# Gate and up as a 2x2x2 block product with seven products, and a down projection that is fed through DRAM

## The chip, the cores and the metric

The kernel runs on one core of a Trainium2 chip. The metric is the device time of one execution in microseconds (us); a lower one is better. The engines are TensorE (PE, matmuls), VectorE (DVE), ScalarE (ACT), GpSimd (POOL) and SyncE (SP, which here only issues DMAs). Each runs its own instructions in order, and they wait for each other by semaphores.

## The reference

One layer of a hybrid decoder, for a batch of one, 1024 tokens, width 1024, in float32. An input projection feeds four heads of a gated delta rule and four heads of differential attention; both results go through one output projection and are added to the residual x. Then comes the feed-forward part that the change is about:

```
x2  = x + concat(la, diff) @ w_out
h   = rmsnorm(x2, ffn_norm_w)
gu  = h @ w_gate_up                 # 1024 x (2 * 2816): gate, then up
act = silu(gu[:, :2816]) * gu[:, 2816:]
x3  = x2 + act @ w_down             # 2816 x 1024
out = rmsnorm(x3, final_norm_w)
```

## The kernel before

Every float32 matrix product is made of three matmuls on operands that are split into a rounded high part and the low rest (`mm3`: high by high, high by low, low by high). The high part is a cast on ACT, the low part a subtraction on DVE, in some places on POOL in two halves (`split`).

The hidden width of 2816 is 22 blocks of 128, called f here. Tokens are eight blocks of 128, called t; k counts eight blocks of the width of 1024; u and n are halves of 512 columns.

Ahead of the FFN: the output projection is done in units of 128 tokens by 512 columns (`out_unit`, 12 matmuls and one DVE sum into the residual, L769). The residual x2 lies in SBUF for all tokens, loaded from x in four DMAs of 1 MB (L796). The units of the delta heads (16) and the diff units of the tokens 4 to 7 are woven into the attention by `fill`, a generator which the attention code asks for matmuls where PE would wait. The diff units of the tokens 0 to 3 follow after the attention (`unit_d`). Each finished half of a token block is squared on ACT (`half_h`), the normalised row block xn is made by two DVE scalings (L1044), transposed by PE and split into `hT_h` and `hT_l` (`trans_h`, L189).

The FFN: `gate_up(f)` loads 128 columns of gate and of up, splits them and does 48 matmuls for each, over all eight k and both halves of the tokens, into two 1024-wide PSUM tiles (`big`). Then come Silu on ACT, the product with up on DVE (L1114) and the split of the result (L1116, L1117), which stays in SBUF. After each group of f blocks (one, then nine twos and a last three; `cuts`) the down products of that group are done: for each t and n, three matmuls per f into a 512-wide PSUM tile (`sm` or `fl`, taken in turn, two buffers each), and a DVE sum into x2 (L1141). In the last group the final norm follows each token block.

PSUM has two `big`, two `sm` and two `fl` buffers. SBUF tiles come from named pools with a number of buffers, so an instruction that fills a buffer waits for the last reader of what was in it. DMAs are issued by SP, in order.

## Time and profile before

| | |
|---|---|
| median of three runs | 1415.88 us (1414.29 to 1417.27) |
| profiled execution | 1417.17 us, of which the span is 1415.5 us |
| mean granted PE clock | 0.987 of full speed |
| busy PE, DVE, ACT, POOL | 1356.0, 665.5, 417.2, 146.7 us |
| matmuls and transpositions on PE | 6804 |
| HBM read, written | 83.48 MB, 18.88 MB |

The span is the part between the first and the last instruction. A busy time is the union of an engine's instructions. Matmuls overlap in the pipeline, so their distance from start to start says what one costs, not the duration in its row. In rows of groups, "idle before" is the time that the engine stood still just before these instructions, with what ended it.

### The profile page before, as it was taken

To read this page: it belongs to the slowest core of one execution; us is meant where nothing else is said; L and a number is where in the kernel's file an instruction comes from. 1 tells how busy PE (TensorE), PEld (TensorE's weight loads), DVE (VectorE), ACT (ScalarE), POOL (GpSimd) and SP (SyncE) were. 2 spreads that over 40 slices of the span, in tenths; PEclk is the share of its full clock that TensorE was granted. 3 is DMA by queue.
4 is the path that set the end of the run, shared out by engine and by line. 5 is a ranking of instruction groups with operands and counts; after the bars stand their busy time and mean duration, and the time that the engine had idled before them with its cause. 6 is when DMAs were issued, how large, how long until landed. Compare 5 with 4: busy or idle time off the path is not lost.

```text
span 1415.5 us, 16570 instructions
## 1 busy us (share of the span) xinstructions
PE 1356.0 (96%) x6804; PEld 1138.5 (80%) x6804; DVE 665.5 (47%) x1071; ACT 417.2 (29%) x758; POOL 146.7 (10%) x124
## 2 busy tenths in 40 slices
...
DMA packets 109108, 103.43 MB, mean 73 GB/s; under 512 B 12096, under 2 KB 89192, under 8 KB 109032
## 3 DMA queue, kind: packets, MB, share of 16 engines
...
q14 instruction: 23, 0.19, 0.0%
HBM read 83.48 MB, written 18.88 MB: 72 GB/s over the span
## 4 chain that ended last, share of the span: by engine, by line
PE 78%; DVE 9%; DMA 5%; issue 3%; ACT 2%; POOL 2%; SPq 0%; POOLq 0%; DVEq 0%; ACTq 0%
PE big L142 15%; PE big L143 15%; PE big L144 15%; PE fl L142 5%; PE fl L144 5%; PE fl L143 5%; PE sm L144 3%; PE sm L143 3%; PE sm L142 3%; DMA ks<-cv 2%; DMA w_raw<-in_w_out 1%; DVE tmp L507 1%; DVE av L509 1%; PE fl L542 1%; DVE mx L888 1%
## 5 line engine op out<-in xcount | busy, mean ns | idle before, releaser
L142 PE MATMUL big<-hT_h,w_h 128*128 128x512 f32 x704 | 274.0, 389 | 0.0
L144 PE MATMUL big<-hT_h,w_l 128*128 128x512 f32 x704 | 273.9, 389 | 0.0
L143 PE MATMUL big<-hT_l,w_h 128*128 128x512 f32 x704 | 273.9, 389 | 0.0
L149 ACT CAST w_h<-w_raw 128x1024 fp32r<-128x1024 f32 x76 | 79.9, 1053 | 404.6 <-PE big L143 223.2
L143 PEld LDWEIGHTS big<-hT_l,w_h 128*128 128x128 f32 x704 | 132.2, 188 | 27.4
L142 PEld LDWEIGHTS big<-hT_h,w_h 128*128 128x128 f32 x704 | 132.2, 188 | 27.3
L144 PEld LDWEIGHTS big<-hT_h,w_l 128*128 128x128 f32 x704 | 132.2, 188 | 27.3
L151 DVE TENSOR_TENSOR w_l<-w_raw,w_h 128x1024 fp32r<-128x1024 f32 x56 | 69.5, 1240 | 156.6 <-ACT w_h L149 138.3
L142 PE MATMUL big<-xT_h,w_h 128*128 128x512 f32 x320 | 127.5, 398 | 0.7 <-DVE cv L433 0.7
L144 PE MATMUL big<-xT_h,w_l 128*128 128x512 f32 x320 | 127.0, 398 | 0.5 <-DVE w_l L151 0.5
L143 PE MATMUL big<-xT_l,w_h 128*128 128x512 f32 x320 | 126.3, 395 | 0.0
L1114 DVE TENSOR_TENSOR cv<-big,cv 128x1024 f32<-128x1024 f32 x22 | 26.9, 1224 | 206.4 <-PE big L144 206.4
L149 ACT CAST dn_h<-w_raw 128x1024 fp32r<-128x1024 f32 x22 | 23.1, 1052 | 235.8 <-PE sm L144 182.2
L1141 DVE TENSOR_TENSOR x<-fl,x 128x512 f32<-128x512 f32 x88 | 60.6, 689 | 40.9 <-PE fl L144 40.9
L155 POOL TENSOR_TENSOR w_l<-w_raw,w_h 128x512 fp32r<-128x512 f32 x40 | 54.5, 1387 | 243.7 <-ACT w_h L149 243.7
L1141 DVE TENSOR_TENSOR x<-sm,x 128x512 f32<-128x512 f32 x88 | 60.6, 688 | 36.5 <-PE sm L144 36.1
L1149 POOL TENSOR_TENSOR ssn<-ssn,expo 128x1 f32<-128x1 f32 x8 | 4.4, 551 | 702.8 <-DVE ssn L1147 702.8
L142 PEld LDWEIGHTS big<-xT_h,w_h 128*128 128x128 f32 x320 | 60.9, 190 | 13.9 <-issue 2.2
L144 PEld LDWEIGHTS big<-xT_h,w_l 128*128 128x128 f32 x320 | 60.6, 189 | 13.1 <-DVE w_l L151 1.0
L143 PEld LDWEIGHTS big<-xT_l,w_h 128*128 128x128 f32 x320 | 60.6, 189 | 12.2 <-issue 0.2
L142 PE MATMUL fl<-dn_h,av 128*128 128x512 f32 x176 | 69.7, 396 | 0.0
L143 PE MATMUL fl<-dn_l,av 128*128 128x512 f32 x176 | 68.6, 390 | 0.0
...
## 6 DMA issues: line engine op xcount, KB each, us to landing
w_raw<-in_w_gate_up SPq DMA_DIRECT2D x44, 512.0 KB, 3.9
w_raw<-in_w_in SPq DMA_DIRECT2D x24, 512.0 KB, 4.0
w_raw<-in_w_down SPq DMA_DIRECT2D x22, 512.0 KB, 3.6
xt<-in_x SPq DMA_DIRECT2D x8, 512.0 KB, 5.5
ks<-cv ACTq DMA_DIRECT2D x8, 512.0 KB, 12.5
aqh<-qh SPq DMA_DIRECT2D x16, 256.0 KB, 4.9
aql<-ql SPq DMA_DIRECT2D x16, 256.0 KB, 7.3
...
```

The costliest lines, as they stand in the source:

```text
L142: nc.tensor.matmul(ps, lhsT=lh, rhs=rh, start=start, stop=False)
L143: nc.tensor.matmul(ps, lhsT=lh, rhs=rl, start=False, stop=False)
L144: nc.tensor.matmul(ps, lhsT=ll, rhs=rh, start=False, stop=stop)
L149: nc.scalar.copy(out=h, in_=raw)
L151: nc.vector.tensor_tensor(out=l, in0=raw, in1=h.bitcast(F32), op=ALU.subtract)
L155: eng.tensor_tensor(out=l[:, c], in0=raw[:, c], in1=h[:, c].bitcast(F32), op=ALU.subtract)
L507: nc.vector.tensor_tensor(out=tv, in0=B[:, i + 1:, i:i + 1].broadcast_to([P, nr, ncol]), in1=X[:, i:i + 1, :ncol].broadcast_to([P, nr, nco ...
L509: nc.vector.tensor_tensor(out=X[:, i + 1:, :ncol], in0=X[:, i + 1:, :ncol], in1=tv, op=ALU.subtract)
L542: nc.tensor.matmul(ps[:, jj * P:(jj + 1) * P], lhsT=At[:, b0 + jj, :], rhs=Df[:, half * 4 + jj, :], start=True, stop=True)
L888: nc.vector.tensor_reduce(out=mx[:, m:m + 1], in_=s[:, :, :w], axis=AX.XY, op=ALU.max, negate=True)
L1114: nc.vector.tensor_tensor(out=sg, in0=ups, in1=sg, op=ALU.mult)
L1141: nc.vector.tensor_tensor(out=x2[:, t, ns], in0=ps, in1=x2[:, t, ns], op=ALU.add)
```

## The change

**Gate and up.** The two matrices and h are cut into blocks: A11 and A12 are the gate weights for the lower and upper half of k, A21 and A22 the up weights; B has rows for the halves of k and columns for the halves of the tokens. Seven products of half size (`product`, 12 matmuls each: four k by three) stand for eight: A11 by B11, A12 by B21, and five on sums, S1 by T1, S2 by T2, S3 by T3, S4 by B22, A22 by T4. The sums T1 to T4 of h are formed once, in `trans_h`; S1 to S4 of the weights in each f on DVE (`w_sum`), one f ahead (`w_prepare`), and two of the low parts on POOL. Two products are accumulated into the PSUM tile of another; the rest are added on DVE (`add`: u2, u3, and the sums into tg and tu). One `big` tile now holds two 512-wide results, pc and pd.

**Down.** The activation of f is stored to DRAM (`act_dr`), in place of being split. When all 22 are done, `down_load` brings activation and down weights back, splits both, and the down products run in seven chunks of 2, 2, 3, 4, 4, 4 and 3 blocks. The first chunk copies PSUM into x2 on ACT, in the third POOL adds the residual, which comes from DRAM; the final norm in the last chunk is as before.

**Residual.** It is no longer held in SBUF. For each unit of the delta heads 128x512 is loaded from x (`res_load`), added and stored to DRAM (`x2_dr`); the diff units load it for a token block (`x2_load`), add, and `half_h` stores it again. The diff units of the tokens 4 to 7 now run token by token.

The core of the diff:

```diff
...
+    def out_unit(parts, mix, u, t, ps, res):
...
+        nc.vector.tensor_tensor(out=res, in0=ps, in1=res, op=ALU.add)
...
+    def res_load(t, u):
+        xh = late["x2p"].tile([P, 512], F32, name="xh", bufs=4)
+        nc.sync.dma_start(out=xh, in_=x_d[t * P:(t + 1) * P, u * 512:(u + 1) * 512])
+        return xh
...
+    def x2_load(t):
+        x2t[t] = op.tile([P, T], F32, name="avl", bufs=4)
+        nc.sync.dma_start(out=x2t[t], in_=x2_dr[t])
...
-        for t in range(0, NT, 2):
-            nc.sync.dma_start(out=x2[:, t:t + 2, :], in_=x_d[t * P:(t + 2) * P, :].rearrange("(t p) d -> p t d", p=P))
...
+        units = [(t, u) for u in range(2) for t in range(NT)]
+        res = {units[0]: res_load(*units[0]), units[1]: res_load(*units[1])}
+        wd = late["wd"] = []
+        for n, (t, u) in enumerate(units):
...
+            yield from out_unit(w[u], mix_la, u, t, flr(), res[t, u])
+            if n + 2 < len(units):
+                res[units[n + 2]] = res_load(*units[n + 2])
+            if n:
+                pt_, pu = units[n - 1]
+                nc.sync.dma_start(out=x2_dr[pt_][:, pu * 512:(pu + 1) * 512], in_=res.pop((pt_, pu)))
+        nc.sync.dma_start(out=x2_dr[t][:, u * 512:(u + 1) * 512], in_=res.pop((t, u)))
...
+        for t in range(4, NT):
+            if t < NT - 2:
+                x2_load(t + 2)
+            for u in range(2):
+                yield from out_unit(wd[u], mix_d, u, t, flr(), x2t[t][:, u * 512:(u + 1) * 512])
...
+            pool, name, bufs = (wp, "w_raw", 2) if t in (4, 5) else (wpools[1][0], "w_raw", 1) if t == 6 else (op, "avl", 4)
+            xns[t] = pool.tile([P, T], F32, name=name, bufs=bufs)
...
+        nc.sync.dma_start(out=x2_dr[t], in_=x2t.pop(t))
+
+    def parts(h, l, raw, eng):
+        nc.scalar.copy(out=h, in_=raw)
+        eng.tensor_tensor(out=l, in0=raw, in1=h.bitcast(F32), op=ALU.subtract)
...
+        pt = big()
...
+        ptv = pt.rearrange("p (k c) -> p k c", c=P)
+        lo, hi = ptv[:, 0:HALF, :], ptv[:, HALF:NK, :]
+        cs = slice((t % 4) * P, (t % 4 + 1) * P)
+        if t >= 4:
+            f = kept[t] = cvt().rearrange("p (k c) -> p k c", c=P)
+            b12, t3 = f[:, 0:HALF, :], f[:, HALF:NK, :]
+            nc.scalar.copy(out=b12, in_=lo)
+            parts(B22[0][:, :, cs], B22[1][:, :, cs], hi, nc.vector)
+            nc.vector.tensor_tensor(out=t3, in0=hi, in1=b12, op=ALU.subtract)
+            parts(T3[0][:, :, cs], T3[1][:, :, cs], t3, nc.gpsimd)
+            return
+        f = kept.pop(t + 4)
+        f1, f2, f4 = f[:, 0:HALF, :], f[:, HALF:NK, :], scratch()
+        nc.scalar.copy(out=first[0][:, :, cs], in_=ptv)
+        nc.vector.tensor_tensor(out=f1, in0=f1, in1=lo, op=ALU.subtract)
+        nc.vector.tensor_tensor(out=f2, in0=lo, in1=f2, op=ALU.add)
+        nc.vector.tensor_tensor(out=first[1][:, :, cs], in0=ptv, in1=first[0][:, :, cs].bitcast(F32), op=ALU.subtract)
+        nc.vector.tensor_tensor(out=f4, in0=hi, in1=f2, op=ALU.subtract)
+        parts(T1[0][:, :, cs], T1[1][:, :, cs], f1, nc.gpsimd)
+        parts(T2[0][:, :, cs], T2[1][:, :, cs], f2, nc.vector)
+        parts(T4[0][:, :, cs], T4[1][:, :, cs], f4, nc.vector)
...
+    def operand():
+        pool, name = slots[used[0] % 4]
+        used[0] += 1
+        w = pool.tile([P, T], F32R, name=name, bufs=4).rearrange("p (a k c) -> p a k c", a=2, c=P)
+        return w[:, 0], w[:, 1]
...
+    def w_fetch(f):
+        rg = wp.tile([P, NK, P], F32, name="w_raw", bufs=2)
+        nc.sync.dma_start(out=rg, in_=gu_v[:, :, f * P:(f + 1) * P])
+        ru = wpools[1][0].tile([P, NK, P], F32, name="w_raw", bufs=1)
+        nc.sync.dma_start(out=ru, in_=gu_v[:, :, DFF + f * P:DFF + (f + 1) * P])
+        return rg[:, 0:HALF], rg[:, HALF:NK], ru[:, 0:HALF], ru[:, HALF:NK]
+
+    def w_split(raw, eng):
+        hl = operand()
+        parts(*hl, raw, eng)
+        return hl
+
+    def w_sum(a0, a1, alu):
+        r = scratch()
+        nc.vector.tensor_tensor(out=r, in0=a0, in1=a1, op=alu)
+        return r
...
+                yield W
+        a11, a12, a21, a22 = w_fetch(f)
+        W["A11"] = w_split(a11, nc.vector)
+        yield W
+        s1 = w_sum(a21, a22, ALU.add)
+        W["S1"] = w_split(s1, nc.vector)
+        yield W
+        yield W
+        s2 = w_sum(s1, a11, ALU.subtract)
+        s4 = w_sum(a12, s2, ALU.subtract)
+        W["S2"] = w_split(s2, nc.vector)
+        yield W
+        W["S4"] = w_split(s4, nc.gpsimd)
+        yield W
+        W["S3"] = w_split(w_sum(a11, a21, ALU.subtract), nc.gpsimd)
+        yield W
+        W["A12"] = w_split(a12, nc.vector)
+        W["A22"] = w_split(a22, nc.vector)
+        yield W
...
+    def product(ps, w, b, begin):
+        for k in range(HALF):
+            for n, (x, y) in enumerate(((w[0], b[0]), (w[0], b[1]), (w[1], b[0]))):
+                nc.tensor.matmul(ps, lhsT=x[:, k, :], rhs=y[:, k, :], start=begin and k == 0 and n == 0,
+                                 stop=k == HALF - 1 and n == 2, skip_group_check=not begin)
...
+    def gate_up(f, W, nxt):
+        pa, pb, pc, pd = banks()
+        tx, tg, tu = temps()
+        u2, u3 = tx[:, n0], tx[:, n1]
+        product(pa, W["A11"], B11, True)
+        nc.scalar.copy(out=u2, in_=pa)
+        next(nxt)
+        product(pb, W["S2"], T2, True)
+        add(u2, pb, u2)
+        next(nxt)
+        product(pc, W["S3"], T3, True)
+        add(u3, pc, u2)
+        next(nxt)
+        product(pd, W["S1"], T1, True)
+        add(tu[:, n1], pd, u3)
+        next(nxt)
+        product(pa, W["A12"], B21, False)
+        nc.scalar.activation(out=tg[:, n0], in_=pa, func=AF.Silu)
+        next(nxt)
+        product(pd, W["S4"], B22, False)
+        add(tg[:, n1], pd, u2)
+        nc.scalar.activation(out=tg[:, n1], in_=tg[:, n1], func=AF.Silu)
+        nc.gpsimd.tensor_tensor(out=tg[:, n1], in0=tg[:, n1], in1=tu[:, n1], op=ALU.mult)
+        next(nxt)
+        product(pc, W["A22"], T4, False)
+        add(tu[:, n0], pc, u2)
+        nc.vector.tensor_tensor(out=tg[:, n0], in0=tg[:, n0], in1=tu[:, n0], op=ALU.mult)
+        W = next(nxt)
+        nc.sync.dma_start(out=act_dr[f], in_=tg)
+        return W
...
+    x2_load(2)
+    unit_d(1, 0)
+    unit_d(1, 1)
+    trans_h(0)
+    W0["S3"] = w_split(w_sum(a11, a21, ALU.subtract), nc.gpsimd)
+    x2_load(3)
+    unit_d(2, 0)
+    unit_d(2, 1)
+    trans_h(1)
+    s4 = w_sum(a12, a22, ALU.subtract)
+    nc.vector.tensor_tensor(out=s4, in0=s4, in1=a21, op=ALU.subtract)
+    nc.vector.tensor_tensor(out=s4, in0=s4, in1=a11, op=ALU.add)
+    W0["S4"] = w_split(s4, nc.gpsimd)
+    unit_d(3, 0)
+    unit_d(3, 1)
+    trans_h(2)
...
+    product(pc, W0["S3"], T3, True)
+    trans_h(3)
+    product(pd, W0["S4"], B22, True)
+    nc.scalar.copy(out=tg[:, n1], in_=pd)
+    late_operands()
+    nxt = w_prepare(1)
+    product(pa, W0["A11"], B11, True)
+    nc.scalar.copy(out=u2, in_=pa)
+    product(pd, W0["S1"], T1, True)
+    next(nxt)
+    product(pb, W0["S2"], T2, True)
...
+    def down_load(f):
+        pool, nh, nl, bufs = homes[min(f % 9, 4)]
+        out = []
+        for src in (act_dr[f], w_dn[f * P:(f + 1) * P, :]):
+            raw = cvt() if f > 1 and src is not act_dr[f] else wp.tile([P, T], F32, name="w_raw", bufs=2)
+            nc.sync.dma_start(out=raw, in_=src)
+            h = pool.tile([P, T], F32R, name=nh, bufs=bufs)
+            l = pool.tile([P, T], F32R, name=nl, bufs=bufs)
+            parts(h, l, raw, nc.vector)
+            out += [h, l]
+        down[f] = out
+
+    for f in range(1, NF):
+        W = gate_up(f, W, w_prepare(f + 1))
+        if f in (4, 6):
+            down_load(f // 2 - 2)
...
+    close_hp()
...
+    chunks = [(0, 2), (2, 4), (4, 7), (7, 11), (11, 15), (15, 19), (19, NF)]
+    ready = 2
+    for c, (f0, f1) in enumerate(chunks):
+        while ready < f1:
+            down_load(ready)
+            ready += 1
+        ahead = chunks[c + 1][1] if c + 1 < len(chunks) else NF
...
+            if c == 2:
+                xr = cvt()
+                nc.sync.dma_start(out=xr, in_=x2_dr[t])
+                for ns in (n0, n1):
+                    nc.gpsimd.tensor_tensor(out=x2[:, t, ns], in0=x2[:, t, ns], in1=xr[:, ns], op=ALU.add)
...
+                for f in range(f0, f1):
+                    ah, al, dh, dl = down[f]
+                    mm3(ps, ah[:, ts], al[:, ts], dh[:, ns], dl[:, ns], f == f0, f == f1 - 1)
+                if c == 0:
+                    nc.scalar.copy(out=x2[:, t, ns], in_=ps)
+                else:
+                    add(x2[:, t, ns], ps, x2[:, t, ns])
...
+            if t % 2 == 1 and ready < ahead:
+                down_load(ready)
+                ready += 1
...
```

In the order of the built program, three places. First PE in gate and up, one f in the middle. Before, the last matmuls of gate and the first of up, in two `big` tiles:

```order
L142 MATMUL big_6430<-hT_h_5502,w_h_6426 128x512
L143 MATMUL big_6430<-hT_l_5503,w_h_6426 128x512
L144 MATMUL big_6430<-hT_h_5502,w_l_6427 128x512
L142 MATMUL big_6496<-hT_h_5502,w_h_6492 128x512
L143 MATMUL big_6496<-hT_l_5503,w_h_6492 128x512
L144 MATMUL big_6496<-hT_h_5502,w_l_6493 128x512
```

Now, from the end of S3 (operand hT3) over four matmuls of A12 (operand hB1, tile sm) to S1 (hT1):

```order
L1177 MATMUL big_6516<-hT3_h_5591,cv_6492 128x512 x2
L1177 MATMUL big_6516<-hT3_l_5592,cv_6492 128x512
L1177 MATMUL big_6516<-hT3_h_5591,cv_6492 128x512
L1177 MATMUL sm_6517<-hB1_h_5583,cv_6509 128x512
L1177 MATMUL sm_6517<-hB1_l_5584,cv_6509 128x512
L1177 MATMUL sm_6517<-hB1_h_5583,cv_6509 128x512 x2
L1177 MATMUL big_6516<-hT1_h_5587,cv_6423 128x512
L1177 MATMUL big_6516<-hT1_l_5588,cv_6423 128x512
L1177 MATMUL big_6516<-hT1_h_5587,cv_6423 128x512 x2
```

Where before one tile followed the other, S1 now goes to the other half of the `big` tile which S3 has just filled, with four matmuls on another tile between.

Second DVE in the same stage. Before, between the last sum of one group and the first of the next: low parts of weights (L151), the product (L1114) and the low part of the activation (L1117):

```order
L151 TENSOR_TENSOR w_l_6744<-w_raw_6741,w_h_6743 128x1024
L1114 TENSOR_TENSOR cv_6398<-big_6430,cv_6398 128x1024
L151 TENSOR_TENSOR w_l_6801<-w_raw_6798,w_h_6800 128x1024
L1117 TENSOR_TENSOR avl_6481<-cv_6398,av_6480 128x1024
L151 TENSOR_TENSOR w_l_6867<-w_raw_6864,w_h_6866 128x1024
L1114 TENSOR_TENSOR cv_6521<-big_6553,cv_6521 128x1024
L151 TENSOR_TENSOR w_l_6924<-w_raw_6921,w_h_6923 128x1024
L1117 TENSOR_TENSOR avl_6604<-cv_6521,av_6603 128x1024
L1141 TENSOR_TENSOR x2_4270<-fl_6613,x2_4270 128x512
```

Now the operations of one f, from u2 on (L1190 are sums out of PSUM, in turn u2, u3, tu, tg and the last tu; L1082 are low parts, L1145 sums of weights):

```order
L1190 TENSOR_TENSOR av_6385<-fl_6384,av_6385 128x512
L1082 TENSOR_TENSOR avl_6456<-xh_6452,avl_6456 128x512
L1190 TENSOR_TENSOR av_6385<-big_6382,av_6385 128x512
L1190 TENSOR_TENSOR av_6387<-big_6382,av_6385 128x512
L1082 TENSOR_TENSOR avl_6512<-w_raw_6403,avl_6512 128x512
L1190 TENSOR_TENSOR av_6386<-big_6382,av_6385 128x512
L1082 TENSOR_TENSOR cv_6509<-w_raw_6401,cv_6509 128x512
L1145 TENSOR_TENSOR xh_6555<-w_raw_6537 128x512
L1145 TENSOR_TENSOR xh_6586<-xh_6555,w_raw_6535 128x512
L1190 TENSOR_TENSOR av_6387<-big_6382,av_6385 128x512
```

Between the sum tg and the last sum of tu there now stand a low part and two sums of weights, the first of them on a tile `w_raw` that a DMA fills.

Third DVE ahead of the FFN, where the early token blocks are finished. Before (L769 is the residual's sum, L189 the low part of h):

```order
L769 TENSOR_TENSOR x2_4270<-fl_5624,x2_4270 128x512
L1040 TENSOR_SCALAR ssh_5580<-ssh_5580 128x1
L1044 SCALAR_TENSOR_TENSOR xn_5579<-x2_4270,ssh_5580,wb2_4271 128x512 x2
L769 TENSOR_TENSOR x2_4270<-sm_5641,x2_4270 128x512
L1039 TENSOR_TENSOR ssh_5639<-ssh_5639 128x1
L1040 TENSOR_SCALAR ssh_5639<-ssh_5639 128x1
L1044 SCALAR_TENSOR_TENSOR xn_5638<-x2_4270,ssh_5639,wb2_4271 128x512 x2
L189 TENSOR_TENSOR hT_l_5503<-big_5661,hT_h_5502 128x8x128
L769 TENSOR_TENSOR x2_4270<-fl_5672,x2_4270 128x512
L769 TENSOR_TENSOR x2_4270<-sm_5689,x2_4270 128x512
```

Now, one early block with its sums (L770), the sums of h (L1108 to L1111), low parts (L1082) and scalings (L1076):

```order
L770 TENSOR_TENSOR avl_5745<-fl_5813,avl_5745 128x512
L770 TENSOR_TENSOR avl_5745<-sm_5830,avl_5745 128x512
L1108 TENSOR_TENSOR cv_5664<-cv_5664,big_5851 128x512
L1109 TENSOR_TENSOR cv_5664<-big_5851,cv_5664 128x512
L1071 TENSOR_TENSOR ssh_5828<-ssh_5828 128x1
L1110 TENSOR_TENSOR hB1_l_5584<-big_5851,hB1_h_5583 128x8x128
L1072 TENSOR_SCALAR ssh_5828<-ssh_5828 128x1
L1111 TENSOR_TENSOR xh_5860<-big_5851,cv_5664 128x512
L1076 SCALAR_TENSOR_TENSOR avl_5827<-avl_5745,ssh_5828,wb2_4300 128x512 x2
L1082 TENSOR_TENSOR hT2_l_5590<-cv_5664,hT2_h_5589 128x4x128
L1082 TENSOR_TENSOR hT4_l_5594<-xh_5860,hT4_h_5593 128x4x128
L1145 TENSOR_TENSOR xh_5872<-w_raw_5704,w_raw_5706 128x512
```

One block now has six operations more in this place, and a sum of weights (L1145) stands among them.

## Rows read from the trace of the kernel before

**Rows 1.** The page, part 1: busy time, share of the span, instructions of each engine.

```profile
PE 1356.0 (96%) x6804; PEld 1138.5 (80%) x6804; DVE 665.5 (47%) x1071; ACT 417.2 (29%) x758; POOL 146.7 (10%) x124
```

**Rows 2.** Windows: start:end, us, busy (count) of PE, PEld, DVE, ACT, POOL; PEclk; DMA; GB/s.

```profile
750.00:800.00 50.00, 50.00 (x221) 41.12 (x220) 19.16 (x23) 8.15 (x8) 0.00 (x0) 1.00 0.15 43
```

**Rows 3.** The page, part 5: one of three alike groups of gate and up.

```profile
L142 PE MATMUL big<-hT_h,w_h 128*128 128x512 f32 x704 | 274.0, 389 | 0.0
```

**Rows 4.** Waits from 690 on (total us, times, longest); then the timeline at one group start.

```profile
PEld fl L142 <- ACT av L1116: 4.4, 11, 0.4
...
710.31 1.05 ACT L1116 CAST av<-cv 128x1024 fp32r<-128x1024 f32 x1 [0.45 <-DVE cv L1114]
...
711.05 0.39 PE L143 MATMUL big<-hT_l,w_h 128*128 128x512 f32 x1
...
711.41 0.50 PE L142 MATMUL fl<-dn_h,av 128*128 128x512 f32 x1
...
711.75 0.40 PE L143 MATMUL fl<-dn_l,av 128*128 128x512 f32 x1
```

**Rows 5.** Timeline in down: a last matmul and the sum that waits for it.

```profile
902.85 0.39 PE L144 MATMUL sm<-dn_h,avl 128*128 128x512 f32 x1
...
903.28 0.69 DVE L1141 TENSOR_TENSOR x<-sm,x 128x512 f32<-128x512 f32 x1 [0.67 <-PE sm L144]
```

**Rows 6.** Groups by shape, DVE, ACT, POOL: busy us, mean ns | idle before.

```profile
L151 DVE TENSOR_TENSOR w_l<-w_raw,w_h 128x1024 fp32r<-128x1024 f32 x56 | 69.5, 1240 | 156.6 <-ACT w_h L149 138.3 <-PE sm L456 17.5 <-ACT vin L657 0.8
L1141 DVE TENSOR_TENSOR x<-fl,x 128x512 f32<-128x512 f32 x88 | 60.6, 689 | 40.9 <-PE fl L144 40.9
...
L1044 DVE SCALAR_TENSOR_TENSOR xn<-x,ssh,wb 128x512 f32<-128x512 f32 x16 | 11.3, 747 | 4.6 <-POOL ssh L1042 4.5
...
L149 ACT CAST w_h<-w_raw 128x1024 fp32r<-128x1024 f32 x76 | 79.9, 1053 | 404.6 <-PE big L143 223.2 <-issue 170.6 <-DMA w_raw<-in_w_out 4.1
...
L925 ACT COPY apt<-sm 128x512 f32<-128x512 f32 x24 | 14.0, 584 | 9.7 <-PE sm L924 9.6
...
L595 ACT CAST cv<-cv 128x512 fp32r<-128x512 f32 x16 | 10.0, 626 | 0.4
...
L155 POOL TENSOR_TENSOR w_l<-w_raw,w_h 128x512 fp32r<-128x512 f32 x40 | 54.5, 1387 | 243.7 <-ACT w_h L149 243.7
```

**Rows 7.** DMA issues: count, KB each, median us from issue to landing.

```profile
w_raw<-in_w_gate_up SPq DMA_DIRECT2D x44, 512.0 KB, 3.9
...
aql<-ql SPq DMA_DIRECT2D x16, 256.0 KB, 7.3
```

**Rows 8.** Windows ahead of the FFN; columns as in rows 2.

```profile
658.00:668.00 10.00, 8.98 (x55) 7.27 (x55) 9.16 (x18) 6.05 (x13) 1.66 (x3) 1.00 0.01 2
668.00:678.00 10.00, 9.65 (x49) 7.85 (x48) 7.55 (x14) 4.04 (x8) 1.10 (x2) 1.00 0.00 1
```

**Rows 9.** Windows at two stalls of the attention; then DVE's wait at the first.

```profile
523.00:533.00 10.00, 4.85 (x28) 3.76 (x25) 3.36 (x8) 4.46 (x10) 3.88 (x3) 0.83 0.95 345
630.00:640.00 10.00, 10.00 (x42) 8.44 (x42) 3.61 (x9) 3.50 (x10) 1.28 (x1) 0.73 0.01 2
...
532.32 0.69 DVE L769 TENSOR_TENSOR x<-fl,x 128x512 f32<-128x512 f32 x1 [6.24 <-DMA x<-in_x]
```

**Rows 10.** Timeline ahead of the FFN: POOL beside DVE, and a group of transpositions.

```profile
680.57 0.16 DVE L1039 TENSOR_TENSOR ssh<-ssh 128x1 f32<-128x1 f32 x1 [0.79 <-ACT xn L1035]
...
682.47 5.54 POOL L155 TENSOR_TENSOR w_l<-w_raw,w_h 128x512 fp32r<-128x512 f32 x4 [0.83 <-ACT w_h L149]
...
684.14 0.68 DVE L769 TENSOR_TENSOR x<-fl,x 128x512 f32<-128x512 f32 x1
...
685.23 1.04 PE L184 MATMUL big<-ident,xn 128*128 128x128 f32 x8
...
686.02 0.48 PE L142 MATMUL big<-hT_h,w_h 128*128 128x512 f32 x1
...
686.91 1.12 DVE L1039 TENSOR_TENSOR ssh<-ssh 128x1 f32<-128x1 f32 x1 [0.79 <-ACT xn L1035]
```

170 lines of the change are left out of this document (83 added, 87 removed).

## The prediction

> **What bounds the kernel now.** I read the page's engine shares first: TensorE (PE) is busy for 1356.0 of 1415.5 us, VectorE (DVE) for less than half of that [rows 1]. Then the table of windows over the FFN: in 50 us PE is busy for 50.00, at the full granted clock, in 221 matmuls [rows 2]. So matmuls of 128x512 start 50 / 221 = 0.2262 us apart; the duration of 0.39 us in the group's row overlaps with the next one, so I count intervals. The FFN is thus paid for by the matmul. It has 2112 matmuls in gate and up (three groups like [rows 3], 704 each) and 1056 in down. What DVE, ScalarE (ACT), GpSimd (POOL) and the DMAs do there is hidden, except in one place: at each of the 11 group starts the down matmuls wait for the cast of the last activation [rows 4].
>
> **What the change removes.** Seven products of 12 matmuls stand for 96 matmuls in each of the 22 f blocks: 84 x 22 = 1848, so 264 fewer. 264 x 0.2262 = **59.7 us** [rows 2, 3]. The down stage keeps its 1056. The 11 waits go too, since the activation now comes long before down starts. Each is an interval of 0.36 where 0.23 is usual, with 0.34 for the next one, so 0.13 + 0.11 = 0.24 us, and 11 of them are **2.7 us** [rows 4].
>
> **What it adds in each f block.** The PE order in the section on the change is S2, S3, then 4 matmuls of A12, S1, 8 of A12, S4, 4 of the next A11, A22, 8 of the next A11. S1 writes the other half of the tile that the sum u3 reads, and A22 writes the half that stands beside the one read for tg; each waits for that DVE sum with four matmuls between. A DVE sum starts 0.43 us after the start of the matmul it waits for [rows 5] and takes 0.69 [rows 6], and PE follows an engine by about 0.05 (the cast of [rows 4] ends at 711.36, the matmul starts at 711.41): 1.17. The matmul before and four fillers give 5 x 0.2262 = 1.13. PE loses 0.04, and the first matmul after a wait has an interval 0.11 longer [rows 4]. That is 0.15 us twice in 21 f blocks: **+6.3 us** (0 if the start is not slow, 12 if each sum comes 0.15 later). S4 has eight fillers, so it waits for nothing.
>
> The period is then 84 x 0.2262 + 0.3 = 19.3 us. DVE has 15 operations of 0.69 in it, 10.3; ACT some 6; POOL two subtractions of 1.39 and a product like them, 4.2 [rows 6]. None is a bound. But DVE runs in order. Let 0 be the start of the eight A11 matmuls; A22's weight part is done on DVE near 15.0, and only then can the up weights of the block after next be loaded, since they have one buffer. Landing takes 3.9 us [rows 7], so the sum s1 runs at about 19.1. Behind it stand s2, the up sum, a weight part, the product, s4, S3, a part, u2 and a part, ten operations or 6.9 us, and then u3, which may start at 19.3 + 7.5 = 26.8. The load may therefore take 4.8 us and cost nothing. I take 0 for that. Two blocks (f = 4 and 6) also load and split operands of down, through the two buffers of the gate weights: 2 x 1 us by half a landing left uncovered each, **+2 us** (0 to 6).
>
> **What it adds ahead of the FFN.** From the first transposition of h to the first A11 product PE has 8 output units of 12 matmuls (21.7 us), 8 groups of transpositions at 0.79 (the interval to the next matmul in [rows 10]; 6.3) and two products (5.4): 33.4 us. Before, DVE was busy for 9.16 and 7.55 of 10 us in it, and PE lost 1.02 and 0.35 [rows 8]. Now each late block takes 2 x 0.69 on DVE (4 blocks: 5.5); each early one two residual sums (1.38), two scalings (1.49), small ones (0.3), one part of 1.24 and five of 0.69, 7.86 (4 blocks: 31.4); the first f's weight sums and part take 5 x 0.69 = 3.4 [rows 6]. That is 40.3 us: DVE becomes the bound, by 6.9. Beside it POOL has 10 subtractions, 13.9 us. The trace shows what these do to DVE: while POOL ran four from 682.47 to 688.01, the small sum L1039, which takes 0.16 elsewhere, took 1.12 and ended at 688.03, while a sum that reads PSUM took its usual 0.68 [rows 10]. A hold of 0.96 at most; at half of it for each of the ten, 4.8. Sum **+12 us**. Low end 4, if DVE does a part of this earlier, where it waits; high end 20, with full holds (9.6) and the chain after the last unit (scalings, transposition, parts: 8.5 us, of which two products hide 5.4) on top.
>
> The Trainium skill has a rule for that row: by "SBUF — State Buffer", "Who interferes with whom", a VectorE instruction with two SBUF inputs and a GpSimd instruction that reads SBUF exclude each other for the whole instruction. The trace agrees with its 1.12 us. By the rule alone every one of the ten could hold DVE for a full 1.39 us, 13.9 in place of 4.8, which would make the time 1384.
>
> **What it moves.** The residual came in four loads of 1 MB; DVE, with the softmax behind it, waited 6.24 us for the first, PE was busy for 4.85 of 10 us there and the clock fell to 0.83 [rows 9]. Now sixteen loads of 256 KB come one by one. But the first stands on SP behind the weight fetches of the output projection, which wait for POOL, so the first sum may be as late as now. Gain 8 at most (5.2 idle and 3 of clock), loss 3; I take **-3**. Stores and reloads of x2 and of the activations (some 12 MB each way for the latter) lie in a stretch where the DMA engines are used for 0.15 of the time [rows 2].
>
> The down stage repeats 1056 matmuls at the old interval, 238.9 us. Its first chunk is tight on ACT: 16 copies out of PSUM at 0.58 and four casts of 1.05, in order, so a cast that waits for a landing holds the copies behind it; four PSUM buffers of 1.36 us each cover 5.4. In the third chunk POOL adds the residual, 16 sums near 1.39 in 32.6 us, and DVE's sums wait for them. No row shows this stage: **+4 us**, one landing; ends 0 and 12, three landings.
>
> **Sum.** -59.7 - 2.7 + 6.3 + 2 + 12 - 3 + 4 = -41.1. The profiled execution took 1417.17 us and would take 1376; it lies 1.3 above the median of 1415.88, so I predict **1375 us**.
>
> **The rivals.**
> A. The new work is hidden: sums come in time, DVE does the first f's work earlier and the x wait vanishes (terms 3, 0, 4, -8, 0): 1353 to 1364. For it: DVE is idle for half of the span. Against: its work is bunched just where PE has least to cover it.
> B. The new stages cost more: ahead of the FFN 20, down 12, inserted loads 6: 1395. For it: two of these stages have no row in the trace, and the full hold is a measured one. Granted clock belongs here: after the stall at 620 it stood at 0.73 in 10 us, a mean of its two levels, 2.4 and 1.2 GHz [rows 9], and gaps ahead of the FFN could do that again.
> C. Slower than before: the up weights come late in every f block. Each us over 4.8 costs 21 us. At the 7.3 us that a 256 KB load took beside others [rows 7] it is 21 x 2.5 = 52, so 1427; it turns into a loss from a landing of 6.9 us. For it: one buffer, and two other transfers of 512 KB in each f. Against: 3.9 us is the median over 44 such loads, and the engines are mostly idle.
> D. POOL holds DVE right ahead of u3 and of tg in each f: 2 x 0.96 x 21 = 40, 1415, no change. Against: POOL's three operations start after u3, tu and tg end, so a hold falls on sums that nobody waits for yet.
>
> **How the numbers follow.** Forecast 0.61 (1366 to 1385), A 0.12, B 0.19, C 0.04, D 0.04. The range goes from 1358, inside A, to 1400, past B. A measurement of this kernel can tell 0.2% (2.8 us) from no change; C gives slower with 0.04, D half of no change and B's far end the rest, 0.03; faster is left with 0.93.
>
> **What would show it.** In the windows inside gate and up, PE at the full clock, 7 products in 19.3 us, and the two waits of PE for DVE named u3 and tg, some 40 in all, near 0.1 us each. If the period is 19.0, the gap term is wrong; if it is above 20, the largest wait of DVE names the culprit: a DMA of the up weights (C) or POOL (D). Between the first transposition and the first A11 product DVE should be busy almost throughout while PE has some 12 us of gaps. In the down stage ACT and POOL should show up as what PE or DVE waits for only in the first three chunks. The prediction is wrong as a whole if the matmul interval in the new products isn't 0.2262.

## The result, and the profile after

| | before | after |
|---|---|---|
| median, us | 1416.49 (1414.29 to 1417.27, 4 runs) | 1379.11 (1377.38 to 1381.21, 4 runs) |
| ratio | | 0.974 [0.972, 0.976] |
| profiled execution, us (span) | 1417.17 (1415.5) | 1377.38 (1375.5) |
| mean granted PE clock | 0.987 | 0.988 |

The changed kernel is 2.6% faster; 1375 was forecast, in a range from 1358 to 1400. The profiled executions differ by 39.8 us, where the sum gave 41.1.

The page of the kernel after, part 1, which answers to [rows 1]:

```profile
PE 1305.1 (95%) x6540; PEld 1086.2 (79%) x6540; DVE 768.1 (56%) x1282; ACT 497.1 (36%) x948; POOL 262.5 (19%) x211
```

PE has 264 instructions fewer and is busy for 51 us less; the other three do some 300 us more work between them. The windows of the kernel after, in gate and up (first) and in down (last); columns as in [rows 2]:

```profile
750.00:800.00 50.00, 50.00 (x218) 40.08 (x217) 27.14 (x41) 18.01 (x29) 10.29 (x8) 1.00 0.34 106
...
1200.00:1250.00 50.00, 50.00 (x222) 41.41 (x221) 21.37 (x27) 9.33 (x10) 0.00 (x0) 1.00 0.19 64
```

PE's busy column reads 50.00 of 50.00 in both, and yet gate and up get 218 matmuls through where down gets 222. A busy share can't show this, since a matmul that starts late still overlaps with the last one; the count does. The waits of the kernel after in gate and up, in columns of total us, times and longest, name what holds them:

```profile
DVE xh L1145 <- DMA w_raw<-in_w_gate_up: 41.9, 19, 3.5
...
PEld big L1177 <- DVE av L1190: 15.0, 40, 1.6
```

The weight load of a product waits for DVE's sum 40 times: S1 and A22, in each of 20 f blocks. The first line is idle time of DVE, which alone costs nothing. Here is one such wait of PE in the timeline of the kernel after (start, duration): the four fillers on `sm`, the sum tg on DVE, and A22's first matmuls on `big`:

```profile
771.86 0.39 PE L1177 MATMUL big<-hB_h,cv 128*128 128x512 f32 x1
772.08 0.39 PE L1177 MATMUL sm<-hB_h,cv 128*128 128x512 f32 x1
...
772.54 0.61 PE L1177 MATMUL sm<-hB_h,cv 128*128 128x512 f32 x2
773.10 0.50 PE L1177 MATMUL big<-hT_h,avl 128*128 128x512 f32 x1
773.44 0.40 PE L1177 MATMUL big<-hT_l,avl 128*128 128x512 f32 x1
...
772.36 0.69 DVE L1190 TENSOR_TENSOR av<-big,av 128x512 f32<-128x512 f32 x1 [0.90 <-PE big L1177]
```

The four fillers end the row at 772.08 + 4 x 0.2267 = 772.99; the sum ends at 773.05, and A22 starts at 773.10. That is 0.11 late, and its 12 matmuls then take 2.85 us (773.10 to 775.95) and not 2.72.

Ahead of the FFN the kernel after loses time. Its windows there, where [rows 8] had PE nearly full:

```profile
680.00:690.00 10.00, 6.10 (x29) 4.29 (x28) 9.26 (x17) 5.27 (x10) 3.54 (x4) 1.00 0.16 64
690.00:700.00 10.00, 5.62 (x23) 3.98 (x22) 8.69 (x14) 4.69 (x8) 2.05 (x3) 0.87 0.14 52
700.00:710.00 10.00, 10.00 (x44) 8.23 (x43) 7.85 (x12) 5.49 (x9) 1.61 (x1) 0.96 0.36 106
...
720.00:730.00 10.00, 7.62 (x27) 5.91 (x26) 5.14 (x8) 2.48 (x4) 1.27 (x1) 0.83 0.16 59
```

PE stands still for 8 of 20 us from 680 on, and again at 724. The waits of PE in the first of these stretches, from the timeline of the kernel after (the bracket is the idle time and what ended it):

```profile
682.23 0.63 PE L1093 MATMUL big<-ident,avl 128*128 128x128 f32 x4 [1.61 <-DVE avl L1076]
687.73 0.50 PE L1177 MATMUL big<-hB_h,cv 128*128 128x512 f32 x1 [1.66 <-ACT cv L1081]
689.09 0.73 PE L1177 MATMUL big<-hB_h,cv 128*128 128x512 f32 x2 [0.63 <-POOL cv L1082]
692.98 1.06 PE L1093 MATMUL big<-ident,avl 128*128 128x128 f32 x8 [1.33 <-DVE xh L1111]
695.15 0.50 PE L1177 MATMUL sm<-hB_h,avl 128*128 128x512 f32 x1 [1.10 <-ACT hB_h L1107]
697.60 0.80 PE L1177 MATMUL sm<-hB_l,avl 128*128 128x512 f32 x1 [1.95 <-DVE hB_l L1110]
```

Six waits, and DVE, ACT and POOL are each named: the last one to arrive is another engine each time.

### The profile page after: what moved, and what is told of

Read it like the earlier page. It is cut to its first block, busy times and chain, and to the rows that moved or that the text cites. A ratio compares the mean times of both kernels' runs of the same rounds, so it can differ in the third digit from the quotient of the medians.

```text
span 1375.5 us, 17042 instructions
## 1 busy us (share of the span) xinstructions
PE 1305.1 (95%) x6540; PEld 1086.2 (79%) x6540; DVE 768.1 (56%) x1282; ACT 497.1 (36%) x948; POOL 262.5 (19%) x211
## 4 chain that ended last, share of the span: by engine, by line
PE 70%; DVE 13%; DMA 5%; issue 4%; ACT 4%; POOL 3%; SPq 1%; POOLq 0%; DVEq 0%; ACTq 0%
PE big L1177 17%; PE sm L1177 8%; PE fl L144 4%; PE fl L145 4%; PE fl L146 4%; PE fl L1177 4%; PE big L144 3%; PE big L145 3%; PE big L146 3%; PE sm L144 3%; PE sm L146 3%; PE sm L145 3%; PE sm L961 1%; DVE tmp L509 1%; DMA ks<-cv 1%
## 5 line engine op out<-in xcount | busy, mean ns | idle before, releaser
L1190 DVE TENSOR_TENSOR av<-big,av 128x512 f32<-128x512 f32 x88 | 60.5, 689 | 109.3 <-PE big L1177 109.2
L1177 PE MATMUL big<-hT_h,cv 128*128 128x512 f32 x264 | 90.8, 405 | 2.4 <-DVE av L1190 2.4
L1177 PE MATMUL big<-hT_h,avl 128*128 128x512 f32 x264 | 89.2, 399 | 1.1 <-DVE av L1190 1.1
L151 ACT CAST w_h<-w_raw 128x1024 fp32r<-128x1024 f32 x32 | 33.5, 1051 | 110.5 <-PE big L145 94.7
L1177 PEld LDWEIGHTS big<-hT_h,cv 128*128 128x128 f32 x264 | 50.4, 191 | 20.2 <-DVE av L1190 9.8
L1177 PEld LDWEIGHTS big<-hT_h,avl 128*128 128x128 f32 x264 | 49.5, 188 | 18.1 <-DVE av L1190 8.0
L1177 PE MATMUL sm<-hB_h,avl 128*128 128x512 f32 x176 | 58.8, 395 | 1.1 <-ACT hB_h L1107 1.1
L1082 POOL TENSOR_TENSOR avl<-xh,avl 128x512 fp32r<-128x512 f32 x23 | 30.8, 1338 | 148.2 <-ACT avl L1081 148.2
L1190 DVE TENSOR_TENSOR x<-fl,x 128x512 f32<-128x512 f32 x48 | 33.0, 687 | 45.6 <-PE fl L146 45.6
L1190 DVE TENSOR_TENSOR x<-sm,x 128x512 f32<-128x512 f32 x48 | 33.0, 687 | 44.8 <-PE sm L146 44.1
L1177 PE MATMUL sm<-hB_h,cv 128*128 128x512 f32 x176 | 57.9, 389 | 0.0
L919 ACT ACTIVATE ae<-big,mx 128x128 f32<-128x128 f32 (+7 forms) x64 | 47.3, 741 | 27.7 <-DVE mx L910 11.6
L1082 POOL TENSOR_TENSOR cv<-xh,cv 128x512 fp32r<-128x512 f32 x22 | 28.3, 1288 | 146.3 <-ACT cv L1081 146.3
L1145 DVE TENSOR_TENSOR xh<-w_raw 128x512 f32<-128x512 f32 x45 | 31.0, 689 | 45.1 <-DMA w_raw<-in_w_gate_up 45.1
L435 DVE SCALAR_TENSOR_TENSOR cv<-big,convw,cv 128x1023 f32<-128x1023 f32 (+2 forms) x36 | 46.0, 1278 | 15.0 <-ACT cv L433 14.4
```

Of the source, the lines that this page charges most:

```text
L151: nc.scalar.copy(out=h, in_=raw)
L435: nc.vector.scalar_tensor_tensor(out=acc[:, d:], in0=ps[:, :T - d], scalar=convw[:, ct, 3 - d:4 - d], in1=acc[:, d:], op0=ALU.mult, op1=AL ...
L919: nc.scalar.activation(out=e[:, :n].rearrange("p (b c) -> p b c", b=nb), in_=s[:, :, :w], func=AF.Exp, bias=mx[:, m:m + 1], accum_out=zs[: ...
L1082: eng.tensor_tensor(out=l, in0=raw, in1=h.bitcast(F32), op=ALU.subtract)
L1145: nc.vector.tensor_tensor(out=r, in0=a0, in1=a1, op=alu)
L1177: nc.tensor.matmul(ps, lhsT=x[:, k, :], rhs=y[:, k, :], start=begin and k == 0 and n == 0, stop=k == HALF - 1 and n == 2, skip_group_check ...
```

## The experiments

The theory after the result: the gaps in gate and up come from S1 and A22 sharing a `big` tile with S3 and S4, and the stretch ahead of the FFN is set by DVE's sum of work. Rivals: the landing of the up weights sets the period; POOL, or the order of the work, sets the stretch. The verdicts go by medians beside runs of the kernel before on the same chip (medians 1415.5 to 1415.8; beside the change itself it was 1416.5), so a difference of 1 us between two of them says nothing.

**A tile for each product.** In `gate_up`:

```diff
-        pa, pb, pc, pd = banks()
+        pa, pb, pc, pd = sma(), flr(), big()[:, 0:512], big()[:, 0:512]
```

> Edit to the changed kernel: in gate_up (f 1 to 21) the two half results pc and pd lie in two big tiles, not in the halves of one. If the short gaps in each f block are the two waits on one tile (S1 for the sum u3, A22 for the sum tg), then the distance from one S2 product to the next falls from 19.48 us to 84 x 0.2267 = 19.05, and the time by 21 x 0.43 = 9 us, to 1370. If PE loses its 0.44 us per f to something else (weight loads of other operands, DVE being late), the distance stays near 19.4 and the time within 2 us of the changed kernel's 1379.

Measured: 1364.12 us (1362.61 to 1364.73), ratio 0.963 [0.962, 0.965], 15.0 less than the change itself. The window in gate and up of this kernel:

```profile
750.00:800.00 50.00, 50.00 (x222) 41.32 (x221) 28.52 (x43) 16.78 (x27) 10.86 (x9) 1.00 0.30 98
```

222 matmuls, as in down, and no wait of PE is listed there any more. The order of the built program changed with the edit too: the products now run whole, one after another, S1 directly behind S3 without the four fillers, and still S1 doesn't wait. From one S2 to the next it takes 19.04 us in nearly every f, which is 84 x 0.2267, where the change itself takes 19.45 to 19.50. That is 20 blocks by 0.43 or 0.44, some 8.8 us. Two things more go with it: the first f after the stretch takes 19.47 instead of 23.48 (4.0), and the block with an inserted down load 19.07 instead of 21.36, which is 1.9 beyond the 0.44 already counted. Both had come through the same wait: a late operand delays a DVE sum, and PE stands only because the next product goes to the tile that this sum reads. With a tile of its own, PE has the whole of a product and more to cover it.

**POOL's ten subtractions ahead of the FFN on DVE.**

```diff
-            parts(T3[0][:, :, cs], T3[1][:, :, cs], t3, nc.gpsimd)
+            parts(T3[0][:, :, cs], T3[1][:, :, cs], t3, nc.vector)
...
-        parts(T1[0][:, :, cs], T1[1][:, :, cs], f1, nc.gpsimd)
+        parts(T1[0][:, :, cs], T1[1][:, :, cs], f1, nc.vector)
...
-    W0["S3"] = w_split(w_sum(a11, a21, ALU.subtract), nc.gpsimd)
+    W0["S3"] = w_split(w_sum(a11, a21, ALU.subtract), nc.vector)
...
-    W0["S4"] = w_split(s4, nc.gpsimd)
+    W0["S4"] = w_split(s4, nc.vector)
```

> Edit to the changed kernel: ahead of the first A11 product the ten subtractions on POOL (parts of T1, T3 and of the first S3 and S4) go to DVE. If DVE's own work paces this stretch, 10 x 0.69 = 6.9 us more of it make the time 4 to 7 us longer, 1383 to 1386. If what costs there is POOL (the power for the norm stands behind its subtractions, DVE idle 1.41 us at 689.4; holds of DVE), the time gets shorter by 1 to 4 us, 1375 to 1378.

Measured: 1383.42 us (1381.76 to 1384.88), 4.3 more. Its windows there:

```profile
680.00:690.00 10.00, 6.94 (x25) 4.63 (x24) 9.90 (x19) 5.30 (x11) 0.55 (x1) 0.83 0.15 62
690.00:700.00 10.00, 5.42 (x23) 3.85 (x24) 10.00 (x17) 5.03 (x8) 0.55 (x1) 0.89 0.20 81
700.00:710.00 10.00, 8.68 (x20) 5.89 (x19) 5.33 (x8) 3.18 (x6) 1.27 (x1) 0.50 0.21 59
```

DVE is now full for 20 us, and the time is what DVE as the bound would give. But the trace doesn't show that it was the bound in the change itself. Nine of the ten subtractions, 5.4 us at 0.60 each, are done before the first A11 product, and that product starts only 1.3 us later (38.66 us after the transposition that waits at 657, against 37.36): most of them went where DVE had idled (5.9 us of that stretch in the change, 2.5 here). The larger loss stands behind it, between the first matmul of A11 and that of S2: 14.51 us against 9.29, with a wait of 1.19 us for a cast on ACT and a granted clock of 0.50 in the third window, PE's lower level of 1.2 GHz (20 matmuls in 10 us, where the change itself has 44).

**The up weights loaded twice**, from the third block on (the first copy is overwritten by an equal one):

```diff
-        nc.sync.dma_start(out=ru, in_=gu_v[:, :, DFF + f * P:DFF + (f + 1) * P])
+        for _ in range(2 if f > 1 else 1):
+            nc.sync.dma_start(out=ru, in_=gu_v[:, :, DFF + f * P:DFF + (f + 1) * P])
```

> Edit to the changed kernel: from f = 2 on the up weights are loaded twice into the same buffer, one load after the other. The rival of late up weights says that a landing of up to 4.8 us is free and each us more costs 20 to 21 us: two loads of 4.0 take about 8, so 20 x 3.2 = 64 us, 1443, slower than before, with a distance of about 22.6 us between S2 products. If the loads have much more slack than I worked out, the time stays within 5 us of 1379.

Measured: 1387.96 us (two runs, 1387.07 and 1388.85), 8.8 more and not 64. Here are SP's issue of the first copy and DVE's sum that needs them, in the timeline of this kernel:

```profile
913.91 0.37 SPq L1136 DMA_DIRECT2D w_raw<-in_w_gate_up  x1
...
921.61 0.69 DVE L1146 TENSOR_TENSOR xh<-w_raw 128x512 f32<-128x512 f32 x1 [1.08 <-DMA w_raw<-in_w_gate_up]
...
926.06 0.68 DVE L1191 TENSOR_TENSOR av<-big,av 128x512 f32<-128x512 f32 x1
```

From the first issue to the sum it takes 7.7 us, 2.9 beyond the 4.8 that I had allowed, and the period is near 19.95, not 22. The test isn't clean: the order of the built program changed with it, three DVE operations now stand in front of s1, and seven with s1 itself run until u3, not ten. But the price of rival C falls: a landing that late cost 0.5 us per f here.

**Both together**, a tile for each product and the up weights twice:

```diff
-        pa, pb, pc, pd = banks()
+        pa, pb, pc, pd = sma(), flr(), big()[:, 0:512], big()[:, 0:512]
...
-        nc.sync.dma_start(out=ru, in_=gu_v[:, :, DFF + f * P:DFF + (f + 1) * P])
+        for _ in range(2 if f > 1 else 1):
+            nc.sync.dma_start(out=ru, in_=gu_v[:, :, DFF + f * P:DFF + (f + 1) * P])
```

> Edit to the kernel of e1: the up weights are loaded twice from f = 2 on, as in e3. If late up weights reach PE through the sum u3 and the shared tile alone, S1 doesn't wait for u3 here and the second load costs almost nothing: up to 3 us over 1364. If they reach PE by the weight operands themselves, it costs as much as in e3, 9 us.

Measured: 1368.73 us (two runs, 1366.78 and 1370.68), 4.6 more than with one load, between the two expectations. In the steady blocks almost nothing is left of the 8.8: most take 19.04 us, a few up to 19.82. What remains falls in the first blocks; that of f = 1 takes 23.02 us, where the two-tile version takes 19.47. There late up weights reach PE by another way than the shared tile, as PE's wait in this kernel shows:

```profile
730.11 0.50 PE L1178 MATMUL big<-hB_h,avl 128*128 128x512 f32 x1 [2.07 <-DVE av L1191]
```

This is product S4. It is accumulated into the tile of S1, which the sum into tu has to read first, and that sum stands on DVE behind s1, which waits 4.00 us for the up weights (727.33).

**The down stage alone**, on the kernel before: activations stored to DRAM and loaded back, in chunks of 1, 1, 2, 3, 4, 4, 4 and 3 blocks; gate, up and the residual as they were.

```diff
-        ah, al = opt("av", F32R), opt("avl", F32R)
-        nc.scalar.copy(out=ah, in_=sg)
-        nc.vector.tensor_tensor(out=al, in0=sg, in1=ah.bitcast(F32), op=ALU.subtract)
+        nc.sync.dma_start(out=act_dr[f], in_=sg)
...
+    chunks = [(0, 1), (1, 2), (2, 4), (4, 7), (7, 11), (11, 15), (15, 19), (19, NF)]
...
+                for f in range(f0, f1):
+                    ah, al, dh, dl = down[f]
+                    mm3(ps, ah[:, ts], al[:, ts], dh[:, ns], dl[:, ns], f == f0, f == f1 - 1)
```

> Edit to the kernel before: only the down projection becomes a stage of its own, fed through DRAM, with eight products in gate and up and the residual in SBUF as before (chunks of 1, 1, 2, 3, 4, 4, 4, 3 for room). It drops the 11 group waits (2.7 us) and adds what the trace of the changed kernel shows as lost in down, 1.5 us: 1413 to 1418, no change. If the down stage were where the gain or a large loss lies, it would differ by more than 5 us.

Measured: 1412.83 us (1411.78 to 1415.39, 10 runs), ratio 0.9981 [0.9972, 0.9990], so 2.7 less. That agrees with the 2.7 us of the 11 group waits [rows 4], which its trace no longer shows; whatever the round trip through DRAM costs is within the interval, 1.3 us.

**The residual in sixteen loads alone**, on the kernel before:

```diff
-        for t in range(0, NT, 2):
-            nc.sync.dma_start(out=x2[:, t:t + 2, :], in_=x_d[t * P:(t + 2) * P, :].rearrange("(t p) d -> p t d", p=P))
...
+            nc.sync.dma_start(out=x2[:, t, us], in_=x_d[t * P:(t + 1) * P, us])
...
+            if n + 2 < len(units):
+                res_load(*units[n + 2])
```

> Edit to the kernel before: the residual comes in sixteen loads of 256 KB, two units ahead, in place of four of 1 MB; nothing else is changed. If this is what brought the changed kernel to the end of the attention 2.7 us earlier than before, the time falls by 2 to 4 us, to 1412 to 1414. If those were other things in the schedule, no change, within 1.5 us.

Measured: 1416.07 us (11 runs), ratio 1.0003 [0.9994, 1.0012]. The pieces are worth nothing by themselves. In this trace DVE's wait for the residual falls from 6.24 us [rows 9] to 2.30, but PE still stands for 3.81 us at this stall, for ACT.

**The weight fetch of the output projection later**, on the two-tile version: the take of the second pair of weights, and the fetches behind it, three units later.

```diff
-        w.append(take_o(0, 1, nc.gpsimd))
-        fetch_o(1, 0, 0)
-        fetch_o(1, 0, 1)
...
+            if n == 3:
+                w.append(take_o(0, 1, nc.gpsimd))
+                fetch_o(1, 0, 0)
+                fetch_o(1, 0, 1)
```

> Edit to the kernel of e1: in the attention the split of the second half of the output weights (cast on ACT, two subtractions on POOL, and the fetches behind it) is asked for after three units of the output projection, not ahead of all. If the first stall of the attention (PE idle for 3.9 us from 524.9 on) is ACT waiting with that cast for its load while the softmax stands behind it, it goes: 3 to 6 us less than 1364, 1358 to 1361. If it is the residual's load or DVE that PE waits for there, the time stays within 2 us of 1364.

Measured: 1364.07 us (1363.23 to 1367.21); the two-tile version took 1364.12. The timeline of the change itself at this stall, then of this experiment:

```profile
526.25 1.04 ACT L151 CAST w_h<-w_raw 128x1024 fp32r<-128x1024 f32 x1 [3.77 <-DMA w_raw<-in_w_out]
...
528.72 0.39 PE L904 MATMUL big<-ak,aqh 128*128 128x256 f32 x1 [3.68 <-ACT ae L919]
...
534.60 0.69 DVE L770 TENSOR_TENSOR xh<-fl,xh 128x512 f32<-128x512 f32 x1 [2.06 <-DMA xh<-in_x]
```

```profile
531.15 0.69 DVE L770 TENSOR_TENSOR xh<-fl,xh 128x512 f32<-128x512 f32 x1 [6.78 <-DMA xh<-in_x]
...
533.64 1.09 PE L947 MATMUL sm<-ident,ae 128*128 128x128 f32 x4 [6.55 <-DVE rz L929]
```

In the first, ACT waits for a weight of the output projection, with the softmax's exponential (`ae`) queued behind it, and PE waits for that. In the second ACT's wait is down to 0.58 us, and DVE waits for the residual instead, with the softmax's `rz` behind it. The order on DVE changed with the edit: in the change `rz` ran at 528.70, ahead of the residual's sum. So one wait went and another came in its place; what the stall would cost without either isn't shown.

**More of the work ahead of the FFN on POOL**, on the two-tile version: four sums of the first f's weights and the low parts of T4.

```diff
-        parts(T4[0][:, :, cs], T4[1][:, :, cs], f4, nc.vector)
+        parts(T4[0][:, :, cs], T4[1][:, :, cs], f4, nc.gpsimd)
...
-    s4 = w_sum(a12, a22, ALU.subtract)
-    nc.vector.tensor_tensor(out=s4, in0=s4, in1=a21, op=ALU.subtract)
-    nc.vector.tensor_tensor(out=s4, in0=s4, in1=a11, op=ALU.add)
+    s4 = w_sum(a12, a22, ALU.subtract, nc.gpsimd)
+    nc.gpsimd.tensor_tensor(out=s4, in0=s4, in1=a21, op=ALU.subtract)
+    nc.gpsimd.tensor_tensor(out=s4, in0=s4, in1=a11, op=ALU.add)
```

> Edit to the kernel of e1 (two big tiles): ahead of the first A11 product the four weight sums for the first S3 and S4 and the four low parts of T4 go from DVE to POOL. If DVE's work paces this stretch, 8 operations less, at the 0.60 us at which they start one after another in the trace of the changed kernel, give 4 to 5 us less than e1's 1364, so 1359 to 1361. If POOL in its turn is the limit (its subtractions take 1.29 and the power for the norm stands behind them), nothing is gained or up to 4 us is lost.

Measured: 1367.46 us (1366.12 to 1369.01), 3.3 more than the two-tile version, not 3 to 5 less. Timeline of this kernel, POOL, then DVE and PE:

```profile
679.78 1.28 POOL L1082 TENSOR_TENSOR hT_l<-cv,hT_h 128x512 fp32r<-128x512 f32 x1 [1.03 <-ACT hT_h L1081]
681.01 1.27 POOL L1145 TENSOR_TENSOR xh<-w_raw 128x512 f32<-128x512 f32 x1
682.24 0.55 POOL L1074 TENSOR_TENSOR ssh<-ssh,expo 128x1 f32<-128x1 f32 x1
682.75 1.26 POOL L1250 TENSOR_TENSOR xh<-xh,w_raw 128x512 f32<-128x512 f32 x1
684.10 1.59 POOL L1251 TENSOR_TENSOR xh<-xh,w_raw 128x512 f32<-128x512 f32 x1
...
682.82 3.42 DVE L1076 SCALAR_TENSOR_TENSOR avl<-avl,ssh,wb 128x512 f32<-128x512 f32 x2 [1.64 <-POOL ssh L1074]
...
684.71 1.09 PE L1093 MATMUL big<-ident,avl 128*128 128x128 f32 x4 [4.39 <-DVE avl L1076]
```

The power function of the norm (L1074), which is POOL's too, stands behind two long operations; DVE's scalings (L1076) wait 1.64 us for it, PE's transposition for these. And the two scalings then take 3.42 us in place of 1.41 (690.82 in the change has 1.42), beside two of POOL's added sums: DVE is held 2.0 us there. So DVE's sum of work isn't the whole story, and the hold that the prediction priced is real where such operations meet.

**Order against amount**, on the two-tile version: the three sums and the split for S4 one token block earlier.

```diff
+    s4 = w_sum(a12, a22, ALU.subtract)
+    nc.vector.tensor_tensor(out=s4, in0=s4, in1=a21, op=ALU.subtract)
+    nc.vector.tensor_tensor(out=s4, in0=s4, in1=a11, op=ALU.add)
+    W0["S4"] = w_split(s4, nc.gpsimd)
     x2_load(3)
     unit_d(2, 0)
```

> The two-tile version (1364.12), with the three weight sums of S4 for the first f and its split moved one token block ahead, in front of the output units of block 2. The same work on the same engines. If the stretch ahead of the FFN is bound by the order in which DVE's work stands (product S4 waits 2.06 and 1.03 us for its cast and its low part, which stand behind these sums), those 3.1 us go and nothing takes their place: 1361. If DVE's sum of work is the bound, the gap comes back at another wait in the same stretch: 1364, within 1 us.

Measured: 1366.25 us (1365.11 to 1366.37), 2.1 more than the two-tile version and above both expectations. PE's waits in this kernel:

```profile
684.05 1.94 PE L1093 MATMUL big<-ident,avl 128*128 128x128 f32 x8 [3.85 <-DVE avl L1076]
693.96 1.23 PE L1093 MATMUL big<-ident,avl 128*128 128x128 f32 x8 [0.77 <-DVE avl L1076]
```

The two waits of product S4 are gone, and the transposition at 684.05 waits 3.85 us in place of 1.60. The gap came back one step earlier, and larger.

**One subtraction of POOL on DVE**, on the two-tile version:

```diff
-    W0["S4"] = w_split(s4, nc.gpsimd)
+    W0["S4"] = w_split(s4, nc.vector)
```

> The two-tile version (1364.12), with one of POOL's ten subtractions ahead of the FFN, the low part of S4 for the first f, on DVE. The power function of the third early block, for which DVE idles 1.4 us, then stands behind one subtraction on POOL, not two. If POOL's queue in front of that function is what costs, 1.2 us less: 1363. If the sum of DVE's work is the bound there, 0.6 us more: 1364.7. In the version with all ten on DVE it was 4.3 more, 0.4 for each.

Measured: 1363.51 us (1362.21 to 1365.13); the runs overlap with those of the two-tile version, so this says neither. The windows of this kernel, then of the two-tile version, then of that version with the up weights twice, which does the same work ahead of the FFN:

```profile
690.00:700.00 10.00, 6.95 (x22) 4.84 (x21) 8.81 (x14) 4.01 (x7) 2.35 (x3) 0.69 0.16 52
700.00:710.00 10.00, 10.00 (x37) 8.07 (x36) 6.90 (x10) 5.21 (x10) 1.61 (x1) 0.79 0.37 106
```

```profile
690.00:700.00 10.00, 5.62 (x22) 4.02 (x21) 8.93 (x14) 4.93 (x8) 1.98 (x4) 0.85 0.14 52
700.00:710.00 10.00, 10.00 (x44) 8.21 (x43) 8.08 (x12) 5.68 (x10) 1.46 (x1) 0.98 0.36 106
```

```profile
690.00:700.00 10.00, 6.92 (x23) 4.75 (x22) 8.35 (x13) 4.16 (x7) 2.28 (x3) 0.68 0.16 52
700.00:710.00 10.00, 10.00 (x38) 8.05 (x37) 6.91 (x10) 5.23 (x10) 1.62 (x1) 0.81 0.36 106
```

DVE's wait for the power function, 1.41 us in the two-tile version, is 0.50 here. But the granted clock is 0.69 and 0.79 where it was 0.85 and 0.98, and from the first matmul of A11 to that of S2 it takes 10.55 us and not 9.23. That can't be put down to the edit: the third kernel has the wait of 1.41 and the waits of S4 as the two-tile version has them, and yet a clock of 0.68 and 0.81, and 10.53 us. So the clock alone moved this part by 1.3 us between two profiled executions of the same work, which is as much as the edit was to give.

## Why the prediction was right, step by step

Each term, in us, by the same points of both traces; the measured ones sum to the 40.0 by which the spans differ. The misses, up to 3.6, nearly cancel, so that the total comes within 1.1 of the forecast is partly luck:

| term | predicted | measured |
|---|---|---|
| 264 matmuls less | -59.7 | -59.9 (0.2267 each) |
| group waits of the FFN | -2.7 | -3.3 |
| two short fillers per f | +6.3 | +8.6 |
| inserted down loads | +2 | +1.9 |
| ahead of the FFN, with the first two f | +12 | +15.6 |
| attention and residual | -3 | -4.4 |
| down stage | +4 | +1.5 |

**Matmuls and waits.** The interval holds for the new products; this term decided the result. The down stage alone gave 2.7 too, within 1.3.

**Fillers.** The mechanism was right, down to the 40 waits; the size was 0.44 per f and not 0.30. For S1 the sum starts 0.43 after its last matmul (763.93 against 763.50) and PE loses 0.04, as worked out. For tg it starts 0.50 after (772.36 against 771.86), so A22 is 0.11 late. And a product after such a wait takes 0.13 to 0.15 longer, not 0.11, since not only its second matmul is slow. The two-tile experiment shows the cause: one tile for two results.

**Up weights.** One step failed here: the slack of 4.8 us. I summed DVE's durations, but they overlap, as two rows of the kernel after show:

```profile
684.47 0.68 DVE L770 TENSOR_TENSOR avl<-fl,avl 128x512 f32<-128x512 f32 x1
685.07 0.68 DVE L1250 TENSOR_TENSOR xh<-xh,w_raw 128x512 f32<-128x512 f32 x1
```

They start 0.60 apart, not 0.69. Ten of them take 6.0. And in a steady block the load was issued at 909.74 and s1 started at 913.81, 4.1 us later and 19.1 after the A11 matmuls, as I said, while DVE idles 1.33 us ahead of u3 (921.67; in the block before it is 2.03, at 902.20): a landing of some 5.4 to 6 us would have been free, by the block. I had counted intervals for PE and durations for DVE. The same error made rival C look nearer than it was. Of the two blocks with an inserted down load only one pays, and it pays the whole 1.9 us (21.36 from S2 to S2; the other takes 19.50).

**Ahead of the FFN.** The size was near, the composition not. Between the first transposition (651.46) and the first A11 product (695.15) PE lost 10.3 us, and 3.9 more inside that product, which took 6.57 us and not 2.72 (2.2 of waiting, the rest at a lower clock). Less some 2 us that the kernel before lost here too, that is close to the 12 forecast, but by luck. But DVE was busy for 35.2 of these 43.7 us, not nearly throughout, and its 62 instructions come to 35 and not 40.3, again because of the overlap; so DVE exceeds PE's 33.4 by 2, not 7. The largest hold beside POOL in this stretch was small: the sum L1071 took 0.65 instead of 0.16 at 663.35. So of the two terms of the sum, 6.9 for DVE and 4.8 for holds, the trace shows about 2 and 0.5. By the rule of the Trainium skill that I weighed ("SBUF — State Buffer", "Who interferes with whom") each of POOL's ten operations could have held DVE in full; here the trace has the remainder of one, and moving all ten to DVE made it slower. With more sums on POOL the trace agrees with the rule: DVE's scalings were held for 2.0 us.

Three things that I had not priced, or only in the high end, stand in their place. POOL's order: the power function of the last early block (690.24) stood behind two subtractions (687.75 and 689.00), and DVE idled 1.41 us. The chain after the last unit: scalings, transposition, cast and low part (the waits at 692.98, 695.15 and 697.60), which the two products ahead hid only in part. And the first f: its successor's up weights were issued at 716.49, and the sum u3 stood behind them:

```profile
716.49 0.37 SPq L1135 DMA_DIRECT2D w_raw<-in_w_gate_up  x1
...
721.32 0.69 DVE L1145 TENSOR_TENSOR xh<-w_raw 128x512 f32<-128x512 f32 x1 [1.95 <-DMA w_raw<-in_w_gate_up]
...
723.97 0.68 DVE L1190 TENSOR_TENSOR av<-big,av 128x512 f32<-128x512 f32 x1
...
724.70 0.79 PE L1177 MATMUL big<-hT_h,cv 128*128 128x512 f32 x1 [2.38 <-DVE av L1190]
```

That is rival C's mechanism, in one block of 22, and it cost 4.0 us: 2.4 of waiting and the rest in clock, 0.83 from 720 on. The experiments don't give the whole stretch one bound. More work on DVE costs 4.3, more on POOL 3.3, another order 2.1, each moves the wait to another place, and the clock alone moves the stretch by 1.3 in the profiled executions. What could be saved there in all stays open.

**Residual.** The value was near, the reason wrong. I read DVE's 6.24 us at 532.32 [rows 9] as what PE waited for. In the kernel before, ACT's cast of an output weight waits 4.15 us at the same place, with the exponential behind it:

```profile
528.36 1.04 ACT L149 CAST w_h<-w_raw 128x1024 fp32r<-128x1024 f32 x1 [4.15 <-DMA w_raw<-in_w_out]
...
530.82 0.58 PE L882 MATMUL big<-ak,aqh 128*128 128x256 f32 x1 [4.05 <-ACT ae L897]
```

PE is idle there from 526.8 to 530.8, and all but 1.02 us of the residual's wait (PE at 533.06) is hidden beside it. In the change PE is idle for 3.68 us up to 528.72, nearly as long, and the pieces alone gave nothing. Of the -4.4, 1.7 stood already before the first changed instruction, so it isn't the change's. The other 2.7 fall partly on a stall at 620, shorter by 1.5; its cause I did not find.

**Down stage.** Neither of the two effects that I priced at 4 occurs where I put it. PE waits once, in the third chunk:

```profile
1168.52 1.75 DVE L1082 TENSOR_TENSOR w_l<-cv,w_h 128x1024 fp32r<-128x1024 f32 x1 [3.23 <-ACT w_h L1081]
...
1170.93 0.50 PE L144 MATMUL sm<-av 128*128 128x512 f32 x1 [0.93 <-DVE x L1190]
```

DVE's sums into x stand behind the low part of a down weight whose cast on ACT waits for its landing (6.90 us up to 1167.43). That is the mechanism that I had for ACT's copies in the first chunk, on DVE and two chunks later; POOL's residual sums add at most the 0.5 us by which the low part is longer than the 1.23 at 1160.56. The first chunk's casts held PE nowhere.
